# A row-sum kernel whose first load is split over even and odd partitions

## The chip, the core and the metric

The kernel runs on one core of a Trainium2 chip. The metric is device time in microseconds (us) of one execution; where several executions are given, their median counts. Lower is better. One further execution was recorded by the hardware profiler, and all views below come from that one.

## The reference

```python
def setup_inputs():
    batch, seq, dim = 32, 512, 1024
    return {"x": np.random.randn(batch, seq, dim).astype(np.float32)}

def reference(x):
    return np.sum(x, axis=-1).astype(np.float32)
```

The input is 32 x 512 = 16,384 rows of 1,024 float32 numbers, 67.1 MB. The output has one sum for each row, 64 KB. There is one addition for each number read, so the input has to pass from device memory (HBM) into the on-chip memory once, and little else has to be done.

## The kernel before

The on-chip memory has 128 partitions. Each partition gets 128 rows: `J = 128` columns in the tile `sums`, one for each row. The rows are in two blocks. `x_a`, the first 128 x 16 rows, gives partition p its rows 16p to 16p+15; `x_b`, the remaining 128 x 112, gives it 112 rows in one piece. `rows_from(j, n)` picks n neighbouring rows of every partition out of one of the two, so that a load reads, for each partition, one piece of n x 4 KB that lies in one place in HBM.

All loads are issued by SyncE (SP), in this order:

- seven rows per partition (`FIRST = 7`, columns 112 to 118 of `sums`), 28 KB for each partition, from `x_a`. This is the load that the change touches. `issue_first_load_at_entry` takes the first SP load of the program, if it waits for nothing, and moves it ahead of SP's first drain in the entry block, so ahead of the barrier in which all engines meet;
- seven loads of 16 rows per partition (`BIG = 16`), 64 KB for each partition, into three buffers in turn (`inpool`, `bufs=3`);
- six rows, two rows and one row, the last row in two pieces of 560 and 464 numbers.

VectorE (DVE) sums a whole load in one `tensor_reduce` (`vec`, L152); the 16-row one takes 17.2 us while the next 16 rows take 19.4 us to arrive. Near the end ScalarE (ACT) takes some rows (`act`, L179), and DVE takes others with a form that folds a row in half (`halves`, L166).

Two things hold back the loads that follow the first one. The tile of the second load, `second`, gets a `memset` on DVE first (L213), and because the load writes the same bytes it waits for that. The third load waits, by `hold`, for the sum over the first one:

```python
hold(load, first, "no descriptors of later loads while the first ones start")
```

`hold(inst, until, reason)` adds nothing but a wait for a semaphore. `ready` (L206) is an ACT instruction on one column of a small tile; it makes ACT fetch its table early, and nothing in the kernel before waits for it.

The schedule is the order of the program text (`manual_schedule`). Every buffer is written again when the sum over it has been done, which the framework turns into waits of the SP queue.

Of the kernel before, what the change touches and what calls it, by code (L numbers as in the profile page):

```python
# [100 lines left out]
@with_exitstack  # L101
def kernel(
    ctx: ExitStack,
    tc: tile.TileContext,
    x: bass.AP,
    out: bass.AP,
):
    nc = tc.nc
    nc.at_finalize(issue_first_load_at_entry)
    nc.at_finalize(order_waits)  # L110
    nc.at_finalize(wait_for_the_store_at_the_clear)
    fp32 = mybir.dt.float32
    P = 128
    batch, seq, dim = x.shape
    rows = batch * seq
    J = rows // P
    BIG = 16

    LONG = J - BIG
    rows_in = x.flatten_outer_dims()
    rows_out = out.rearrange("b s -> (b s)")
    x_a = rows_in[: P * BIG].rearrange("(p j) d -> p j d", p=P)
    x_b = rows_in[P * BIG :].rearrange("(p j) d -> p j d", p=P)
    out_a = rows_out[: P * BIG].rearrange("(p j) -> p j", p=P)
    out_b = rows_out[P * BIG :].rearrange("(p j) -> p j", p=P)


    def rows_from(j, n):
        return x_b[:, j : j + n, :] if j < LONG else x_a[:, j - LONG : j - LONG + n, :]

    last = 0
    FIRST = 7
    pieces = (560, 464)
    LINE = 64

    with (
        tc.tile_pool(name="small", bufs=1) as smallpool,  # L140
        tc.tile_pool(name="in", bufs=3) as inpool,
        tc.tile_pool(name="unread", bufs=4, space=bass.MemoryType.PSUM) as upool,
        tc.tile_pool(name="stage", bufs=1) as stpool,
        tc.manual_schedule(),
    ):


        seed = smallpool.tile([P, LINE // 2], fp32)
        sums = stpool.tile([P, J], fp32)

        def vec(dst, src):
            return nc.vector.tensor_reduce(  # L152
                out=dst, in_=src, axis=mybir.AxisListType.X, op=mybir.AluOpType.add
            )

        def hold(inst, until, reason):
            tc.add_manual_dep(
                inst.ins,
                until.ins.name,
                mybir.DependencyInfo(mybir.DependencyClass.Sync, mybir.DependencyReason.DATA),  # L160
                reason=reason,
            )

        def halves(dst, src):
            n = src.shape[-1] // 2
            return nc.vector.tensor_tensor_reduce(  # L166
                out=src[:, :n],
                in0=src[:, :n],
                in1=src[:, n:],
                scale=1.0,  # L170
                scalar=0.0,
                op0=mybir.AluOpType.add,
                op1=mybir.AluOpType.add,
                accum_out=dst,
            )

        def act(dst, src, n):
            unread = upool.tile([P, dim], fp32)
            nc.scalar.activation(  # L179
                out=unread[:, :n],  # L180
                in_=src,
                func=mybir.ActivationFunctionType.Copy,
                accum_out=dst,
            )

        sums_of = []

        def rows(t, a, n, j, n_act, pairs=False):
            nv = n - n_act
            block = t[:, a * dim : (a + n) * dim].rearrange("p (n d) -> p n d", d=dim)  # L190
            load = nc.sync.dma_start(out=block, in_=rows_from(j, n))  # L191
            if pairs:
                for q in range(nv):
                    sums_of.append(halves(sums[:, j + q : j + q + 1], block[:, q, :]))
            else:
                sums_of.append(vec(sums[:, j : j + nv], block[:, :nv, :]))
            for q in range(nv, n):
                act(sums[:, j + q : j + q + 1], block[:, q, :], dim)
            return load

        def store(eng, dst, j0, j1):
            return eng.dma_start(out=dst, in_=sums[:, j0:j1])

        nc.vector.memset(seed[:, :1], 0.0)  # L204
        unread = upool.tile([P, dim], fp32)
        ready = nc.scalar.activation(  # L206
            out=unread[:, :1], in_=seed[:, :1], func=mybir.ActivationFunctionType.Copy
        )

        j = last  # L210
        t = inpool.tile([P, BIG * dim + LINE], fp32)
        second = inpool.tile([P, BIG * dim + LINE], fp32, name="t")
        nc.vector.memset(second[:, : 4 * dim], 0.0)  # L213
        rows(t, 0, FIRST, j, 0)
        first = sums_of[-1]
        wholes = [LONG, *range(BIG, LONG, BIG)]
        for k, at in enumerate(wholes):
            t = second if k == 0 else inpool.tile([P, BIG * dim + LINE], fp32)
            if k < len(wholes) - 1:
                load = rows(t, 0, BIG, at, 0)  # L220
            else:
                rows(t, 0, BIG, at, 7, pairs=True)
            if k == 1:
                hold(load, first, "no descriptors of later loads while the first ones start")

        t = inpool.tile([P, BIG * dim + LINE], fp32)
        rows(t, FIRST, 6, j + FIRST, 2, pairs=True)
        two = rows(t, FIRST + 6, 2, j + FIRST + 6, 1, pairs=True)
        a = BIG - 1

        j += a
        c, width = pieces
        whole = t[:, a * dim + c : BIG * dim + 2]
        nc.vector.memset(whole[:, width + 1 :], 0.0)  # L234
        part = t[:, a * dim : a * dim + c]
        nc.sync.dma_start(out=part, in_=rows_from(j, 1)[:, 0, :c])  # L236
        nc.sync.dma_start(out=whole[:, :width], in_=rows_from(j, 1)[:, 0, c:])
        late = "its packets come behind those of the loads"
        hold(store(nc.scalar, out_b[:, BIG:], BIG, LONG), two, late)
        hold(store(nc.scalar, out_a, LONG, J), two, late)  # L240
        halves(whole[:, width : width + 1], part)
        halves(sums[:, j : j + 1], whole)
        store(nc.sync, out_b[:, :BIG], 0, BIG)
# [30 lines left out]
```

## Time and profile before

| What | Value |
|---|---|
| Time, median of 3 runs | 161.35 us (161.17 to 161.35) |
| Time of the profiled execution | 161.16 us |
| Its span in the profile | 159.4 us |
| DVE busy | 124.1 us (78%) |
| ACT busy | 12.1 us (8%) |
| HBM read | 67.11 MB, mean 421 GB/s over the span |
| First load (seven rows, 3,584 KB) | lands 10.7 us after its issue |

The profiled execution took 161.16 us, of which its span of 159.4 us begins with SP's issue of the first load; 1.8 us lie outside the span. A name such as `t<-in_x_dram` says what is written and what is read. An entry with a q behind the engine (SPq) belongs to that engine's sequencer, which issues DMAs and waits, and not to its arithmetic.

### The profile page before, as it was taken

The numbers are of one execution on the slowest core, as the hardware profiler recorded it, in microseconds if no ns is written. First come the engines' busy times: TensorE is split into PE (matmuls) and PEld (weight loads), VectorE is DVE, ScalarE is ACT, GpSimd is POOL, SyncE is SP. The second block draws the span as 40 slices with busy tenths as digits, with TensorE's granted clock in tenths as the row PEclk, the third lists the DMA queues.
The fourth block names the chain that finished last, engine by engine and source line by source line (L and its number), as shares of the span: only waits on it lengthen the run. The fifth ranks groups of instructions, "written<-read, shape, count | busy, mean of one in ns | idle before, by whom it ended". The sixth has DMA issues, their size and how long they took to land.

```text
span 159.4 us, 137 instructions
## 1 busy us (share of the span) xinstructions
DVE 124.1 (78%) x42; ACT 12.1 (8%) x22; POOL 0.2 (0%) x4
## 2 busy tenths in 40 slices
DVE  5339600499985999779995899949999499994955
ACT  3000000000000000000000000000000000003993
POOL 0000000000000000000000000000000000000000
DMA  9899999699699699699699797996996996995984
GB/s 324 374 486 526 395 395 526 280 510 526 263 526 526 263 526 526 263 526 526 263 526 461 329 526 313 477 526 263 526 526 263 526 526 263 526 526 247 444 371 139
DMA packets 2160, 67.18 MB, mean 421 GB/s; under 512 B 624, under 2 KB 752, under 8 KB 880
## 3 DMA queue, kind: packets, MB, share of 16 engines
q1 hardware_dynamic: 1872, 67.12, 97.9%
q10 hardware_dynamic: 288, 0.06, 0.2%
HBM read 67.11 MB, written 0.07 MB: 421 GB/s over the span
## 4 chain that ended last, share of the span: by engine, by line
DMA 71%; DVE 27%; SPq 1%; issue 0%; DVEq 0%
DMA t<-in_x_dram 71%; DVE sums L152 26%; SPq L191 0%; SPq L236 0%; DVE t L166 0%; DVEq L269 0%
## 5 line engine op out<-in xcount | busy, mean ns | idle before, releaser
L152 DVE TENSOR_REDUCE sums<-t 128x16 f32<-128x16384 f32 (+1 forms) x7 | 110.9, 15849 | 27.9 <-DMA t<-in_x_dram 27.9
L179 ACT ACTIVATE unread<-t 128x1024 f32<-128x1024 f32 x10 | 10.1, 1010 | 144.1 <-DMA t<-in_x_dram 144.1
L166 DVE CUSTOM_DVE_ANT_0 t<-t 128x512 f32<-128x512 f32 (+2 forms) x16 | 9.6, 656 | 4.0 <-DMA t<-in_x_dram 4.0
L213 DVE MEMSET t<- 128x4096 f32 x1 | 3.5, 3472 | 0.8 <-issue 0.8
L179 ACT ACTIVATION_READ_ACCUMULATOR unread<-t 128x1 f32 x10 | 1.9, 186 | 0.0
L206 ACT ACT_TABLE_LOAD x1 | 1.3, 1283 | 0.8 <-PEq L258 0.8
L166 DVE DVE_READ_ACCUMULATOR2_ANT sums<- 128x1 f32 x15 | 1.2, 83 | 0.0
L204 DVE MEMSET seed<- 128x1 f32 x1 | 0.1, 59 | 0.9 <-PEq L258 0.9
L206 ACT ACTIVATE unread<-seed 128x1 f32<-128x1 f32 x1 | 0.2, 174 | 0.0
L258 POOL MEMSET const-bfloat16-1.0<- 128x1 bf16 x1 | 0.1, 102 | 0.0
L258 POOL MEMSET const-uint8-127<- 128x1 uint8 x1 | 0.1, 102 | 0.0
L258 POOL MEMSET const-float32-0.0<- 128x1 f32 x1 | 0.1, 99 | 0.2 <-issue 0.2
L258 POOL MEMSET const-float32-1.0<- 128x1 f32 x1 | 0.1, 99 | 0.0
L166 DVE DVE_READ_ACCUMULATOR2_ANT t<- 128x1 f32 x1 | 0.1, 82 | 0.0
L234 DVE MEMSET t<- 128x1 f32 x1 | 0.1, 59 | 0.0
## 6 DMA issues: line engine op xcount, KB each, us to landing
t<-in_x_dram SPq DMA_DIRECT2D x1, 3584.0 KB, 10.7
t<-in_x_dram SPq DMA_DIRECT2D x1, 3072.0 KB, 28.7
t<-in_x_dram SPq DMA_DIRECT2D x1, 1024.0 KB, 30.8
t<-in_x_dram SPq DMA_DIRECT2D x1, 280.0 KB, 31.0
t<-in_x_dram SPq DMA_DIRECT2D x1, 232.0 KB, 31.1
t<-in_x_dram SPq DMA_DIRECT2D x7, 40.7
out_dram<-sums ACTq DMA_DIRECT2D x1, 48.0 KB, 1.6
out_dram<-sums ACTq DMA_DIRECT2D x1, 8.0 KB, 1.5
```

What stands on the lines that cost most here:

```text
L152: return nc.vector.tensor_reduce(out=dst, in_=src, axis=mybir.AxisListType.X, op=mybir.AluOpType.add)
L166: return nc.vector.tensor_tensor_reduce(out=src[:, :n], in0=src[:, :n], in1=src[:, n:], scale=1.0, scalar=0.0, op0=mybir.AluOpType.add, op ...
L179: nc.scalar.activation(out=unread[:, :n], in_=src, func=mybir.ActivationFunctionType.Copy, accum_out=dst,)
L204: nc.vector.memset(seed[:, :1], 0.0)
L206: ready = nc.scalar.activation(out=unread[:, :1], in_=seed[:, :1], func=mybir.ActivationFunctionType.Copy)
L213: nc.vector.memset(second[:, : 4 * dim], 0.0)
L234: nc.vector.memset(whole[:, width + 1 :], 0.0)
L258: nc = _bacc.Bacc("TRN2", target_bir_lowering=False, num_devices=1)
```

## The change

The load of the first seven rows becomes two: one over partitions 0, 2, 4 and so on, one over partitions 1, 3, 5 and so on, each with 64 pieces of 28 KB. The even one is the first SP load of the program now and waits for nothing, so it is the one that goes ahead of the barrier. The odd one waits for `ready`. The sum over the seven rows stays one instruction over all 128 partitions and so waits for both loads. In SP's order the odd load stands between the even one and the first 16-row load; nothing else moves on any engine.

```diff
         j = last
         t = inpool.tile([P, BIG * dim + LINE], fp32)
+        block = t[:, : FIRST * dim].rearrange("p (n d) -> p n d", d=dim)
+        source = rows_from(j, FIRST)
+        nc.sync.dma_start(out=block[0::2], in_=source[0::2])
+        odd = nc.sync.dma_start(out=block[1::2], in_=source[1::2])
+        hold(odd, ready, "no second load while the first one's descriptors are made")
         second = inpool.tile([P, BIG * dim + LINE], fp32, name="t")
         nc.vector.memset(second[:, : 4 * dim], 0.0)
-        rows(t, 0, FIRST, j, 0)
-        first = sums_of[-1]
+        first = vec(sums[:, j : j + FIRST], block)
+        sums_of.append(first)
         wholes = [LONG, *range(BIG, LONG, BIG)]
```

## The prediction

> **What bounds the kernel now.** I read the page first, for who is busy and which chain ends last.
>
> ```profile
> span 159.4 us, 137 instructions
> DVE 124.1 (78%) x42; ACT 12.1 (8%) x22; POOL 0.2 (0%) x4
> ...
> DMA  9899999699699699699699797996996996995984
> ...
> DMA t<-in_x_dram 71%; DVE sums L152 26%; SPq L191 0%; SPq L236 0%; DVE t L166 0%; DVEq L269 0%
> ```
>
> The chain's 26% of DVE does not make DVE a limit. The sixes in the DMA row come of how packets of 2.4 us fall into slices of 4 us. Windows that are long against a packet show the true rate, and the chain in order of time shows where both ends lie:
>
> ```profile
> 0.00:1.00 1.00, 0.06 (x1) 0.22 (x1) 0.20 (x4) 1.00 0.00 0
> 1.00:2.00 1.00, 0.26 (x1) 1.00 (x1) 0.00 (x0) 1.00 1.67 459
> 30.00:150.00 120.00, 107.14 (x19) 3.82 (x7) 0.00 (x0) 1.00 0.99 427
> ```
>
> ```profile
> 0.00 10.73 DMA t<-in_x_dram
> 10.73 0.02 issue
> 10.75 7.63 DVE sums L152
> ...
> 126.08 31.10 DMA t<-in_x_dram
> 157.18 0.02 issue
> 157.21 0.40 DVE t L166
> ```
>
> The last two columns of the first view are the DMA engines' busy share and GB/s: nothing moves in the first microsecond, then the 16 engines are full (0.99, 427 GB/s). The packet records of the trace say the same more finely. Every packet of the first load but the 16 first ones took 1.062 us for 28,672 bytes, every 16-row packet 2.418 us for 65,536: 27 GB/s an engine, back to back. All load packets together, divided by 16, make 155.8 us, from the first packet at 1.01 us to the last end at 156.8 us. So the time is: start of the first packet, plus 155.8 us of full engines, plus a tail. Only the first term, or a hole in the second, can change. The change works on the first. Three more views give its rows: the tile's instructions in the first microsecond, the same over the whole span, and the timeline.
>
> ```profile
> L191 SPq DMA_DIRECT2D t<-in_x_dram x1: 381/381/381, 0.0 to 0.0; - x1
> ```
>
> ```profile
> L191 SPq DMA_DIRECT2D t<-in_x_dram x10: 327/328/436, 0.0 to 125.1; - x10
> ...
> L236 SPq DMA_DIRECT2D t<-in_x_dram x1: 477/477/477, 125.6 to 125.6; - x1
> ```
>
> ```profile
> 0.78 1.28 ACT L206 ACT_TABLE_LOAD   x1 [0.78 <-PEq L258]
> ...
> 1.74 3.47 DVE L213 MEMSET t<- 128x4096 f32 x1 [0.82 <-issue]
> 2.08 0.17 ACT L206 ACTIVATE unread<-seed 128x1 f32<-128x1 f32 x1
> 10.75 7.62 DVE L152 TENSOR_REDUCE sums<-t 128x7 f32<-128x7168 f32 x1 [5.54 <-DMA t<-in_x_dram]
> ```
>
> The first issue took SP 0.381 us. Of the 16 engines, 15 start their first packet between 1.01 and 1.26 us (one is recorded at 1.88), and all end it between 2.64 and 2.98, 1.46 to 1.93 us after those starts where 1.062 us would do. That is the whole opening: 0.38 us of issue, 0.63 us from its end to the first packet, 0.25 us of spread between engines, some 0.6 us until data flow.
>
> **The change part by part.**
>
> The even load's issue. Every DMA of the trace is over 128 partitions at a step of one, so no row shows an issue over 64 at a step of two. By its nearest row, the first load's own 0.381 us, it costs nothing more; the issue does not look at size (0.327 us for 64 KB a partition, 0.347 for the 64 B of the last store), so a gain from half the bytes has no support. There is a reason for a loss: in the built programs all 15 DMAs of before carry a flag for a ready-made issue (`ant_dge_precooked`), and the two half loads are the only ones of the changed program without it. What that is worth no row shows. I bound it by nothing and by one more issue of the same length, +0.38 us, and take the middle, +0.20 us, all of it on the path, as everything later queues behind the first packet.
>
> Half the descriptors ahead of the first packets. If descriptors are made engine after engine, the spread of 0.25 us is their making, and half of them halves it: the last engine gains 0.12 us, the mean one 0.06. If all must be made before any packet starts, half of the 0.63 us is the end of what could go, -0.32 us. If the delay is fixed, nothing. Against the large value speaks the data flow: the first packets do not end in the order in which they start (one runs from 1.02 to 2.89 us, the last starter from 1.26 to 2.82), so the flow waits for something else than the making. I take -0.06. [...]
>
> One more load. Each engine gets one more completion packet, 9 ns in the records and some 6 ns around it: +0.015 us. When the second load was issued at 5.2 us, the packets running then took up to 1.069 us in place of 1.062; the odd load's descriptors do that once more over two packets: +0.015 us.
>
> The odd load's wait. It is released by `ready` at 2.25 us (later by what the even issue is longer, as SP's drain in the barrier stands behind that issue). With an issue of 0.38 to 0.76 us and 0.63 us to the packet it is there by 3.3 to 3.8 us. The even load keeps the engines busy until 1.0 + 0.6 + 4 x 1.06 = 5.9 us. So the wait costs nothing under a cover of some 2 us; every microsecond beyond it would be a hole in all engines and go to the end in full. Queued behind the waiting instruction on SP is the second load. It waits for the memset that ends at 5.21 us, so it is not moved by an odd issue that is over by 3.2; if the barrier is 0.2 us later, so are the memset and it, and its packets are wanted at 10.05 us. DVE's sum needs both completions and begins where the second comes, near 10.75; it ends near 18.4, and the third load behind it is wanted at 29.4. Both hide under the second load's 19.4 us.
>
> Sum: 0.20 - 0.06 + 0.015 + 0.015 = +0.17 us, from 161.16 us of the profiled execution to 161.33. That execution lies 0.19 us under the median of the runs, 161.35, and a median is what is compared: 161.5. The bounds of the terms, -0.32 + 0.03 and 0.38 + 0.03, give 161.05 to 161.75. A measurement of this kernel can tell about 0.2%, 0.32 us, from no change, so this forecast is "no change that can be told", on its late side.
>
> **The rivals.**
>
> The issue becomes the price (slower). Place: SP's first instruction. If the even load's issue takes 0.75 us or more, the start moves by over 0.32 us even with the 0.06 taken off, and the end with it, as nothing behind the first packet has slack. With an issue of 0.8 to 1.0 us: +0.36 to +0.59 us with the other terms, 161.7 to 161.95. For it: the missing flag, and full engines that cannot catch up. Against: all 15 issues of the trace lie between 0.33 and 0.48 us.
>
> The descriptors were the price (faster). The even load's issue is no longer than 0.38 us, the making is half, and packets had waited for all of it: -0.32 - 0.12 + 0.03 = -0.41 us, 160.95. For it: the opening is the one place where the engines idle. Against: the mixed order of ends, and 0.85 us from issue to first packet even for the last store with its 64 B a partition.
>
> Engines share a way into the partitions (much slower). With steps of two, an engine's four pieces may lie where another engine writes too. Two on one way at 27 GB/s make each of the eight first packets cost 1.062 us more: +8.5 us, 169.85, or half of that, 165.6, if only one of the loads suffers. The trace shows each engine at one steady pace in every load, so the 128-partition layout has no such sharing, and nothing on a step of two. [...]
>
> That nothing happens, with a fixed delay and an equal issue, is +0.03 us and part of the forecast's case.
>
> **How the numbers follow.** Forecast's case, the start moved by less than 0.32 us either way: 0.48. Long issue: 0.34, as the missing flag is the one definite difference between the programs. Descriptors: 0.10. Shared ways: 0.08. So faster 0.10, same 0.48, slower 0.34 + 0.08 = 0.42. The range takes in the first three, 160.9 to 161.95, and leaves out the sharing and the far ends of a long issue. The likeliest case alone: 161.05 to 161.65.
>
> **What would show it.** In the changed kernel's trace: SP's first issue against 0.381 us (0.58 expected; 0.75 or more is the first rival); first packets at 1.1 to 1.3 us with half the spread between engines (the second rival: 0.6 to 0.7 us); eight packets an engine of 1.062 us without a hole at 5.9 us (the third: 2.1 us each); both halves landed near 10.9 us; the later chain the same, shifted as a whole. A hole between the even and the odd packets, or a tail of another length, would make the prediction wrong in a way that I give no chance of its own.

## The result, and the profile after

The changed kernel takes 162.09 us (median of 5 runs, 161.90 to 162.56) against 161.29 us: a ratio of 1.0051 with an interval of 1.0035 to 1.0067. It is slower by 0.8 us, where 0.17 us and "no change that can be told" were forecast, and it lies above the range. One line of the description of the kernel needs setting right first: the kernel has `last = 0`, so the seven rows of the first load are rows 0 to 6 of `x_b` and fill columns 0 to 6 of `sums`; the pieces of 28 KB are as described, and no figure depends on it. The profiled execution took 162.17 us; its page begins:

```profile
span 160.4 us, 140 instructions
DVE 124.2 (77%) x42; ACT 12.1 (8%) x22; POOL 0.2 (0%) x4
...
DMA  7999699699699699699799799798997996996993
...
DMA 70%; DVE 26%; ACT 1%; SPq 1%; issue 0%; DVEq 0%
```

The last line has the shares by engine of the chain that ended last. The busy times are those of before. One entry is new in the chain's shares, ACT with 1%. The chain in order of time, the tile's instructions in the first microsecond, and the timeline show the opening:

```profile
1.19 1.28 ACT L206
2.47 0.01 issue
2.48 0.18 ACT unread L206
2.67 0.01 issue
2.68 8.62 DMA t<-in_x_dram
...
126.86 31.30 DMA t<-in_x_dram
158.16 0.04 issue
158.21 0.40 DVE t L166
```

```profile
L214 SPq DMA_DIRECT2D t<-in_x_dram x1: 549/549/549, 0.0 to 0.0; - x1
```

```profile
2.68 0.48 SPq L215 DMA_DIRECT2D t<-in_x_dram  x1
5.65 0.34 SPq L191 DMA_DIRECT2D t<-in_x_dram  x1
11.40 7.62 DVE L152 TENSOR_REDUCE sums<-t 128x7 f32<-128x7168 f32 x1 [5.78 <-DMA t<-in_x_dram]
```

The even load's issue takes 0.549 us (0.381 before). SP's drain behind it takes 0.362 us (0.132), so the barrier opens 0.40 us later, and `ready` lets the odd load go at 2.68 us. The chain runs through ACT and the odd load now.

The last fold starts at 158.21 us against 157.21, 1.0 us later in this pair of executions. The packet records split that, by the packet that is last at each point:

- The first packet starts at 1.33 us, not 1.01: +0.31 us.
- The seven rows' last packet ends at 11.00 us, not 10.40. So another +0.29 us goes at the boundary: two engines take 1.54 and 1.48 us for their first odd packet in place of 1.06.
- The last 16-row packet ends at 146.72 us, not 145.80: +0.31 us more in the 16-row loads. There 78 of 896 packets take 20 ns or more over 2.418 us, up to 0.13 us more (before: 20, none over 0.03). I call the sum of what all 16-row packets take over 2.418 us, divided by 16 engines, the excess: 0.37 us, against 0.14 before. So the excess explains 0.22 of these 0.31 us; it is an average over the engines, and the last engine lost more.
- Some 0.1 us is left for the loads behind them.

Averaged over the engines instead, the boundary costs only some 0.06 us.

### The profile page after: what moved, and what is told of

It is laid out like the page before. It is cut to its first block, busy times and chain, and to the rows that moved or that the text cites. A ratio compares the mean times of both kernels' runs of the same rounds, so it can differ in the third digit from the quotient of the medians.

```text
span 160.4 us, 140 instructions
## 1 busy us (share of the span) xinstructions
DVE 124.2 (77%) x42; ACT 12.1 (8%) x22; POOL 0.2 (0%) x4
## 4 chain that ended last, share of the span: by engine, by line
DMA 70%; DVE 26%; ACT 1%; SPq 1%; issue 0%; DVEq 0%
DMA t<-in_x_dram 70%; DVE sums L152 26%; ACT L206 1%; SPq L191 0%; SPq L241 0%; DVE t L166 0%; ACT unread L206 0%; DVEq L152 0%; DVEq L274 0%
```

## The experiments

Each kernel was timed against the kernel before on the same chip; "over" is the difference of the medians. Theory A: the longer issue is the price. Its first rival: a second load or its boundary is.

**The issue by itself.** The kernel before, with the flag for the ready-made issue taken from its first load.

```diff
         assert not load.sync_info.on_wait
+        load = copy.replace(load, ant_dge_precooked=False)
```

> The kernel before, with its one first load over all 128 partitions, but without the flag for the ready-made issue on that load. Theory A (the issue is the price): SP's first issue takes about 0.55 us as in the changed kernel (0.381 before), the drain behind it 0.36, the first packet starts near 1.33 us, and the time is 0.3 us over before; what else the changed kernel lost (0.8 us in all) stays away. Theory B (the half partitions and the second load are the price, the flag is worth nothing): 0.381 us, first packet near 1.01, time of before within 0.1 us.

Measured: 161.55 us, 0.31 over (ratio 1.0017, 1.0008 to 1.0026), excess 0.15 us.

```profile
L192 SPq DMA_DIRECT2D t<-in_x_dram x1: 550/550/550, 0.0 to 0.0; - x1
```

The flag is worth 0.17 us of issue, 0.23 us of the drain behind it (0.367 us) and 0.31 us of first packet: 1.33 us here as in the changed kernel. That is theory A, for 0.3 of the 0.8 us. The number of pieces is worth nothing, as 128 pieces without the flag start when 64 do.

**Two loads without partition steps.** Four and three rows over all partitions.

```diff
-        nc.sync.dma_start(out=block[0::2], in_=source[0::2])
-        odd = nc.sync.dma_start(out=block[1::2], in_=source[1::2])
+        nc.sync.dma_start(out=block[:, :4], in_=source[:, :4])
+        odd = nc.sync.dma_start(out=block[:, 4:], in_=source[:, 4:])
```

> Two first loads over all 128 partitions, of four rows and of three, both flagged, the second one waiting for the same ACT instruction as the odd load. Theory A: first issue 0.38 us, first packet near 1.01 us, time within 0.1 us of before. Theory B (a second load at this place costs by itself, at the boundary between the two, where two engines of the changed kernel took 1.5 us in place of 1.06 for their first odd packet): some engines stall by 0.4 us at the boundary, time 0.3 to 0.5 us over before.

Measured: 161.39 us, 0.15 over (0.9998 to 1.0016), first packet at 0.99 us. So a second load with a wait on `ready` is not dear by itself, as theory A had it.

**The changed kernel again, and before again.**

> The changed kernel once more. In its first profile single 16-row packets all over the run took 0.02 to 0.13 us too long, which before did not show, and the last load landed 0.4 us later than the first loads' delay explains. Theory A (these are an accident of that execution): they are not there again, the profile lies nearer to 0.6 us over before, and the median 0.5 to 0.8 over. Theory C (they come from the change, for instance from engines that are out of step): they are there again, at about the same size.

> The kernel before once more, for a second profile of it on the chip of these runs. Theory A: if this chip or hour makes long packets, they are here too, and then belong to no kernel. Theory C: none are here, as in the first profile of before (first packet near 1.01 us, last load landed near 157.2 us).

Measured: 162.10 us, 0.86 over, and 161.20 for before. The excess is 0.68 us in the changed kernel and 0.13 in before, so theory A's "accident" falls: the long packets belong to the change. The timeline of the changed kernel, again, shows them adding up; in brackets is DVE's idle time. Then the same of before:

```profile
30.75 17.22 DVE L152 TENSOR_REDUCE sums<-t 128x16 f32<-128x16384 f32 x1 [11.72 <-DMA t<-in_x_dram]
50.37 17.22 DVE L152 TENSOR_REDUCE sums<-t 128x16 f32<-128x16384 f32 x1 [2.40 <-DMA t<-in_x_dram]
69.92 17.22 DVE L152 TENSOR_REDUCE sums<-t 128x16 f32<-128x16384 f32 x1 [2.33 <-DMA t<-in_x_dram]
89.32 17.22 DVE L152 TENSOR_REDUCE sums<-t 128x16 f32<-128x16384 f32 x1 [2.18 <-DMA t<-in_x_dram]
```

```profile
30.17 17.22 DVE L152 TENSOR_REDUCE sums<-t 128x16 f32<-128x16384 f32 x1 [11.80 <-DMA t<-in_x_dram]
49.42 17.22 DVE L152 TENSOR_REDUCE sums<-t 128x16 f32<-128x16384 f32 x1 [2.03 <-DMA t<-in_x_dram]
68.81 17.22 DVE L152 TENSOR_REDUCE sums<-t 128x16 f32<-128x16384 f32 x1 [2.17 <-DMA t<-in_x_dram]
88.15 17.22 DVE L152 TENSOR_REDUCE sums<-t 128x16 f32<-128x16384 f32 x1 [2.12 <-DMA t<-in_x_dram]
```

From one of these sums to the next, a load takes 19.4 to 19.6 us in place of 19.3 to 19.4.

**Both row-wise loads without the flag.** The two loads of the second experiment; a function run on the built program takes the flag from both (the other loads have other lengths).

```diff
+            if isinstance(i, mybir.InstDMACopy) and i.engine == mybir.EngineType.SP and i.outs[0].ap[1][1] in (4096, 3072):
+                insts[k] = copy.replace(i, ant_dge_precooked=False)
```

> The two first loads of four and of three rows over all 128 partitions, now both without the flag, as the two half loads are. The changed kernel loses 0.3 us by its longer issue and some 0.5 us more, for which its two profiles show 16-row packets that take up to 0.3 us too long. Theory D (the 0.5 us come from the loads over 64 partitions at a step of two): time 0.3 us over the flagged two loads, near 161.7, the 16-row packets at 2.418 us throughout (excess over that, summed over all and divided by 16 engines, about 0.13 us as in before). Theory E (they come from a second load without the flag, issued while the first one runs): near 162.1, excess 0.4 to 0.7 us as in the changed kernel.

Measured: 161.66 us, 0.42 over, excess 0.08 us. The 0.3 us of the issue are there, the long packets are not; theory E falls.

**The wait taken away.**

```diff
         odd = nc.sync.dma_start(out=block[1::2], in_=source[1::2])
-        hold(odd, ready, "no second load while the first one's descriptors are made")
```

> The changed kernel without the odd load's wait, so that it is issued right behind the barrier. Theory D: the wait is not the price, time as the changed kernel, near 162.1, long packets as there. Theory F (the odd load's descriptors come at a bad moment, while the second packets run, and throw the engines out of step): another moment, another loss; time moves by 0.2 us or more either way and the spread between engines at the end of the seven rows changes with it (0.42 to 0.73 us in the two profiles of the changed kernel, 0.35 to 0.38 in before).

Measured: 161.57 us, 0.33 over (1.0013 to 1.0030), excess 0.12 us. Its timeline:

```profile
1.19 0.48 SPq L215 DMA_DIRECT2D t<-in_x_dram  x1
...
30.62 17.22 DVE L152 TENSOR_REDUCE sums<-t 128x16 f32<-128x16384 f32 x1 [11.70 <-DMA t<-in_x_dram]
49.89 17.22 DVE L152 TENSOR_REDUCE sums<-t 128x16 f32<-128x16384 f32 x1 [2.05 <-DMA t<-in_x_dram]
69.22 17.22 DVE L152 TENSOR_REDUCE sums<-t 128x16 f32<-128x16384 f32 x1 [2.10 <-DMA t<-in_x_dram]
```

Issued 1.5 us earlier, the odd load costs nothing beyond the issue: the other 0.5 us are the wait's, which moves the load, as theory F had it in the main. Theory D falls, as the loads over every other partition are all here.

**Halves in place of even and odd.**

```diff
-        nc.sync.dma_start(out=block[0::2], in_=source[0::2])
-        odd = nc.sync.dma_start(out=block[1::2], in_=source[1::2])
+        nc.sync.dma_start(out=block[:64], in_=source[:64])
+        odd = nc.sync.dma_start(out=block[64:], in_=source[64:])
```

> The first load split into partitions 0 to 63 and 64 to 127 in place of even and odd. Theory of shared ways (engines that write to the same eighth of the partitions share one way at 27 GB/s): packets of the first loads take about 2.1 us in place of 1.06, and the time is up to 8.5 us over before; the even and odd split, whose packets kept 1.06 us, is then a layout that avoids it. If no ways are shared: time as the changed kernel, near 162.1.

Measured: 170.33 us (170.22 to 170.34 in three executions, 192.61 in a fourth), 9.1 over. The packets of both loads take 2.24 us at the median. The windows, first of halves and then of the changed kernel, with GB/s last:

```profile
2.00:18.00 16.00, 3.47 (x1) 0.65 (x2) 0.00 (x0) 1.00 0.99 204
```

```profile
2.00:10.00 8.00, 3.47 (x1) 0.64 (x2) 0.00 (x0) 1.00 0.95 405
```

The halves move at half the rate of the even and odd loads, which keep 1.06 us a packet at the median, as the single load of before does. The theory of shared ways forecast about 2.1 us a packet for the halves. That engines share a way was not shown by itself; no other reason for the rate was tried.

**Quarters.** Four loads over every fourth partition, the second with the wait.

```diff
+        nc.sync.dma_start(out=block[0::4], in_=source[0::4])
+        for q in range(1, 4):
+            odd = nc.sync.dma_start(out=block[q::4], in_=source[q::4])
+            if q == 1:
+                hold(odd, ready, "...")
```

> The first load in four over every fourth partition, 32 pieces each, the second one waiting for the ACT instruction, the others behind it. Theory D (a partition step above one sets off the long packets): they are there, time 162.1 or later. Descriptor theory: the first packets start earlier than the 1.33 us of the 64-piece load by up to 0.1 us if the number of pieces is made before they start; if the issue is all, again 1.33 us and 0.55 us of issue.

Measured: 162.30 us, 1.06 over, excess 0.27 us, an issue of 0.54 us and the first packet at 1.33 us. Theory D forecast that time too, but it fell with the run without the wait. Without the flag, 32, 64 and 128 pieces alike have their first packet at 1.33 us.

**The odd load's moment.** A part of the memset (64 or 1,500 columns) releases it. The lead is the time from the issue of a load until the packets of the load before it end.

```diff
+        second = inpool.tile([P, BIG * dim + LINE], fp32, name="t")
+        gate = nc.vector.memset(second[:, :64], 0.0)
         odd = nc.sync.dma_start(out=block[1::2], in_=source[1::2])
-        hold(odd, ready, "no second load while the first one's descriptors are made")
-        second = inpool.tile([P, BIG * dim + LINE], fp32, name="t")
-        nc.vector.memset(second[:, : 4 * dim], 0.0)
+        hold(odd, gate, "no second load while the first one's descriptors are made")
+        nc.vector.memset(second[:, 64 : 4 * dim], 0.0)
```

> The changed kernel with the odd load released by the first 64 columns of the memset on DVE, near 2.2 us, in place of the ACT instruction (issued at 2.7 us in the changed kernel, at 1.2 us without the wait). Without the wait the time was 161.57 us and the long 16-row packets were gone; with it 162.1. Theory J (the odd load must be there some 3.5 us before the even one's packets end near 6.0 us, because the engines read ahead of what they write): a lead of 3.8 us in place of 3.3, so a time between the two, 161.6 to 161.9. Theory K (the wait itself is the price, or any issue while data flow): as the changed kernel, 162.1.

> The same with 1,500 columns of the memset, so that the odd load is issued near 3.5 us. Theory J: a lead of 2.5 us; every engine stalls at the boundary, by 0.3 to 0.8 us, and the time is 162.4 to 162.9. Theory K: 162.1 as the changed kernel, since its packets are wanted only near 6.0 us and 1.9 us pass from issue to flow.

Measured: 161.84 us (0.57 over, excess 0.12, issued at 1.45 us, earlier than I had reckoned) and 162.43 us (1.16 over, excess 0.37, issued at 2.95 us). In both, 0.27 us more than usual lie outside the span (2.06 us against 1.79), which the last section takes up; without them they stand 0.30 and 0.89 over. The issues of the two:

```profile
1.45 0.48 SPq L217 DMA_DIRECT2D t<-in_x_dram  x1
```

```profile
2.95 0.48 SPq L217 DMA_DIRECT2D t<-in_x_dram  x1
```

Theory K falls by the first: the wait has no price of its own, its moment has. The second decides nothing. Only the 0.27 us outside the span put it into theory J's range; its span is that of the changed kernel, 160.4 us, and its lead is nearly the same. Nor did every engine stall: four took 0.19 to 0.33 us too long for their first odd packet, and one stood still for 0.25 us.

**The second row-wise load late.** Four rows, then three, the second load released by the whole memset.

```diff
+        nc.sync.dma_start(out=block[:, :4], in_=source[:, :4])
+        gate = nc.vector.memset(second[:, : 4 * dim], 0.0)
         odd = nc.sync.dma_start(out=block[:, 4:], in_=source[:, 4:])
-        hold(odd, ready, "...")
+        hold(odd, gate, "...")
```

> The two first loads of four and three rows over all 128 partitions with the flag, the second one released by the whole memset, near 5.25 us in place of 2.26. The first one's packets end at 6.3 to 7.1 us in its earlier profile, so the lead is 1.1 to 1.8 us. Theory J: a hole between the two loads of 0.5 to 1 us in all engines and long 16-row packets after it, time 161.9 to 162.5: lateness alone does it, at any partition step. Theory L (only loads at a step of two set off long packets): a hole, but 16-row packets at 2.418 us (excess under 0.15 us) and the time over the 161.39 us of the early release by the hole alone.

Measured: 161.73 us, 0.46 over, excess 0.09 us. In its profiled execution (162.12 us) the loss is at the boundary: packets of the second load take up to 0.62 us too long, 0.37 us an engine on average, and the engines stand still by 0.11 us at most. So there is no hole, which both theories expected. The 16-row packets are clean, which theory J did not expect and theory L did.

**Three tries at the long packets.** A tiny extra load over the even partitions of a spare tile; an extra load into partitions 0 to 7; and four rows over all partitions, followed by three rows over the even and the odd ones.

```diff
+        spare = smallpool.tile([P, 16], fp32)
+        extra = nc.sync.dma_start(out=spare[0::2], in_=rows_from(j, 1)[0::2, 0, :16])
+        hold(extra, ready, "while the first load's packets run")
```

```diff
+        nc.sync.dma_start(out=t[:8, 8 * dim : 9 * dim], in_=rows_from(j, 1)[:8, 0, :])
```

```diff
+        nc.sync.dma_start(out=block[:, :4], in_=source[:, :4])
+        even = nc.sync.dma_start(out=block[0::2, 4:], in_=source[0::2, 4:])
+        hold(even, ready, "while the first load's packets run")
+        nc.sync.dma_start(out=block[1::2, 4:], in_=source[1::2, 4:])
```

> The kernel before with its one first load, and one tiny extra load of 64 B into each even partition of a spare tile (64 pieces, not needed for the result), issued when the ACT instruction is done, while the first load's packets run, as the odd load is in the changed kernel. Theory M (descriptors of a load over every other partition, written while data flow, set off the long packets): excess of the 16-row packets 0.3 us or more, time 161.6 to 161.9. Theory P (they come of how the engines stand to each other after the boundary between even and odd): no boundary with a stall here, excess under 0.15 us, time within 0.1 us of before.

> The kernel before with an extra load of 4 KB into each of partitions 0 to 7, behind the first load and not needed for the result, which puts some of the engines behind the others by 0.15 to 0.6 us. Theory P: the engines stand otherwise to each other than in before, long packets follow, excess 0.3 us or more and the time over before by 0.3 us more than the delay that the end of the first two loads shows. Theory M: no step of two, excess under 0.15 us, the time over before by that delay alone.

> Four rows over all 128 partitions with the flag, then three rows over the even and three over the odd partitions, both issued from 2.3 us on, while the first four rows' packets run until 6.3 us or later. Leads of 3 to 4 us, more than the odd load has in the changed kernel. Theory M: long packets, excess 0.3 us or more, time 161.7 to 162.0. Theory J (lead alone decides): excess under 0.15 us, time near the 161.39 us of the two row-wise loads.

Measured: 161.55 us (0.30 over, excess 0.11), 161.37 us (0.12 over, excess 0.14) and 161.32 us (0.07 over, 0.9997 to 1.0014, excess 0.07). Theory M falls twice: loads over every other partition, issued at 2.26 and 2.84 us while data flow, cost nothing when what runs lasts until 6.5 us. Theory P has no support. The tiny load's 0.30 us was foreseen by neither and stays unexplained. In its profile the engines end the first load's packets 0.66 us apart, against 0.35 in before; they are that far apart from the end of their first packets on, at 2.66 to 3.32 us, and the tiny packets themselves take 0.04 us.

**The lead by itself.** Eleven first rows in place of seven, in the changed kernel and in before (the tail's load of six rows becomes one of two).

```diff
-    FIRST = 7
+    FIRST = 11
```

> The changed kernel with eleven first rows in place of seven (the tail has two rows in place of six to match), so that the even load's packets last until about 8.6 us while the odd load is issued at 2.7 us as before: a lead of 5.9 us in place of 3.3. Theory J (the lead decides): no long packets, excess of the 16-row packets under 0.15 us, time 0.3 us over the single load of eleven rows. Theory Q (issuing the odd load while the even one runs is the price, whatever the lead): long packets, time 0.6 to 0.9 us over the single load of eleven rows.

> The single first load with eleven rows, the measure for the run above. Both theories: near the time of before, 161.2 to 161.5 us, as the tail is short of work on all engines but DMA; excess under 0.15 us.

Measured: 164.56 and 164.19 us, excess 0.09 and 0.12 us. With eleven rows the kernel is slower in itself, against what I expected: in the second run the last data arrive at 156.97 us (156.82 in before), but ACT is busy with its rows until 160.6. What is lost ahead of the last 16-row load still reaches the end, as DVE and ACT wait for it. The pair's difference is 0.37 us. The odd load is issued as in the changed kernel and costs nothing but the issue:

```profile
2.69 0.48 SPq L215 DMA_DIRECT2D t<-in_x_dram  x1
```

At the front nothing else differs from the changed kernel but the length of the pieces, 44 KB in place of 28, and with it how long the even load lasts (until 8.68 us in place of 6.03). Theory Q falls, theory J stands.

**Short leads elsewhere.** The row-wise load and the pair behind four rows, released by a part of the memset (3,200 and 2,600 columns).

```diff
+        gate = nc.vector.memset(second[:, :3200], 0.0)
+        odd = nc.sync.dma_start(out=block[:, 4:], in_=source[:, 4:])
+        hold(odd, gate, "no second load while the first one's descriptors are made")
```

> Four and three rows over all 128 partitions with the flag, the second one issued near 3.9 us, with a lead of some 2.4 us in place of 4.1 (early) or 1.1 (late). Theory J with partial stalls: some engines run dry at the boundary and others not, long packets follow as in the changed kernel, excess 0.25 us or more, time 161.7 to 162.2. Theory R (only loads over half the partitions can do it): excess under 0.15 us, time between the 161.39 of the early and the 161.73 of the late release.

> Four rows over all partitions, then three rows over the even and over the odd ones, issued near 3.4 us in place of 2.3: a lead of some 3.0 us, as short as in the changed kernel. Theory J and theory R: the long packets are there, excess 0.25 us or more, time 161.7 to 162.2 against 161.32 with the early release. Theory Q: as with the early release, 161.3, since both are issued while the first load runs.

Measured: 162.86 us (1.56 over, excess 0.02) and 162.65 us (1.35 over, excess 0.03); 1.29 and 1.08 over without the 0.27 us outside the span. The loads went out at 4.29 and 3.67 us, some 0.3 us later than I had reckoned. The windows of the first of them, then of the same loads released early:

```profile
4.00:10.00 6.00, 1.06 (x2) 0.00 (x0) 0.00 (x0) 1.00 0.98 360
```

```profile
4.00:10.00 6.00, 1.20 (x1) 0.00 (x0) 0.00 (x0) 1.00 1.01 433
```

A short lead is dear with all partitions and the flag, too: single packets of the second load take up to 1.23 us too long, and one engine stands still for 0.63 us. But the loss lies at the boundary, and the 16-row packets are clean. In the second kernel both theories J and R expected long packets, and they are not there either. So a short lead costs time in all the layouts here, as theory J has it in the main, and the form that the cost takes follows neither theory.

The kernels with a second early load, by lead, taken here until the first engine has done with the load before it ("net": without the 0.27 us outside the span). The halves, with another packet rate, and the two extra loads, which carry nothing that is needed, are left out. Issue, lead and excess are of the one profiled execution:

| Kernel | Issued | Lead | Excess | Over before, net |
|---|---|---|---|---|
| even/odd of eleven rows | 2.69 | 6.0 | 0.09 | 0.37 over its single load |
| even/odd, no wait | 1.19 | 5.0 | 0.12 | 0.33 |
| even/odd, 64 columns | 1.45 | 4.7 | 0.12 | 0.30 |
| rows, then even/odd | 2.26 | 4.2 | 0.07 | 0.07 |
| rows, no flag | 2.68 | 4.1 | 0.08 | 0.42 |
| rows | 2.26 | 4.1 | 0.10 | 0.15 |
| **changed kernel** (and again) | 2.68 | 3.3 (3.6) | 0.37 (0.68) | 0.80 (0.86) |
| even/odd, 1,500 columns | 2.95 | 3.2 | 0.37 | 0.89 |
| rows, then even/odd, mid | 3.67 | 2.8 | 0.03 | 1.08 |
| rows, mid | 4.29 | 2.1 | 0.02 | 1.29 |
| quarters | 2.67 | 1.5 | 0.27 | 0.79 |
| rows, late | 5.24 | 1.2 | 0.09 | 0.46 |

With 4.1 us of lead or more, nothing is lost but the 0.3 us of a missing flag on the first load, within 0.15 us. With 3.6 us or less something always is. The layouts on the two sides of that line differ; in one layout alone, even/odd of seven rows, the step lies between 3.6 and 4.7 us.

## Why the prediction was wrong, point by point

**What bounds the kernel** held: full engines from the first packet to the last (a DMA share of 0.99 from 30 to 150 us, before and after), and the losses at the front and in packets reached the end. "Every 16-row packet 2.418 us" is the most frequent value; they take up to 2.446 us in before, which makes its excess of 0.14 us.

**The even load's issue** was the right mechanism and somewhat undersized: +0.20 us was put, with bounds from 0 to 0.38; it is 0.31, shown by the flag alone. The issue itself grew by 0.17; the first packet came another 0.15 us later, from a cause that the records do not show. SP's drain behind the issue grew too, by 0.23 us, and delayed the barrier and with it the odd load.

**Half the descriptors** (-0.06) is nothing. The spread of the first packets, which half the descriptors should have halved, is 0.32 us against 0.25 (one engine left out in each). The faster rival, which needed them to be the price, is out.

**One more load** (two times 0.015 us) was not resolved; the rows-then-even/odd run, with two more loads, is 0.07 us over before and not told from it.

**The odd load's wait** is the step that failed: "the wait costs nothing under a cover of some 2 us". I had put the issue of the odd load at 2.25 us and a bit, its packets "there by 3.3 to 3.8 us" and wanted at 5.9, as if an engine wanted its next packet only when the last one ends. Issued at 2.68 us, the odd load ought by that to have had 1.9 us to spare (2.68 + 1.33 = 4.0 us). The runs show that it has to be issued earlier: leads of 3.3 to 3.6 us lose 0.5 us, leads of 4.7 us nothing. Without the wait the kernel took 161.57 us, inside the range; the wait is what took it out. What I had called a hole "in all engines" was 0.42 and 0.48 us in two engines' packets, and a scatter of long 16-row packets until 144 us. A hole between the even and the odd packets was named as a sign of being wrong, with no chance of its own; for the long packets the prediction had no case.

**The long-issue rival** was not what happened: its point of decision, an issue of 0.75 us, was not reached (0.55), though the start moved by 0.31 us, just under the 0.32 that it names. That the time came out near this rival's (161.7 to 161.95 us) is chance, as 0.5 of the 0.8 us are the wait's. Its +0.36 us, by the other terms, should read +0.39; nothing hangs on that. The sharing rival (+8.5 us) comes near what the halves lose, 9.1 us, and is wrong for this change, whose 28 KB packets keep 1.06 us at the median. Its chance of 0.08 was my estimate; the profile of before has no load at a step of two.

**Left open.** That the odd load's moment decides, and not its wait or its form, is shown by the run without the wait, the eleven-row pair and the load released by 64 columns. How is not. That engines read ahead of what they write, the reason that theory J gives, was my guess; no run showed it. Long 16-row packets (excess 0.27 to 0.68 us) follow a short lead where the first load of all is over half or a quarter of the partitions; where it is over all of them, a short lead costs only at the boundary, even if half loads come next. Why is not explained. Engines out of step are not the reason by themselves: the row-wise load in the middle has a spread of 0.98 us between engines all through its 16-row loads, and no long packets. Nor is it explained why a wholly late load (lead 1.2 us, 0.46 over) costs less than one half late (2.1 us, 1.29 over), nor why an extra load of 64 B a partition costs 0.30 us.

## What to carry to other kernels

Where the DMA engines never rest (a share of 0.99 here), a load that is held back must be issued well before the queue ahead of it runs out: here 4.1 us were enough and 3.6 us were not, in different layouts, though issue and first packet account for only 1.3 us. So judge such a wait by runs at several moments and not by the arithmetic of latencies. A split that changes a load's shape can change the cost of issuing it: for the first load here the issue took 0.55 us in place of 0.38, and the first packet came 0.31 us later; the missing flag alone cost 0.31 us of the time. If a load has to be split by partitions, use every other partition and not the halves (162.09 against 170.33 us here).

## What the runs showed of the hardware

- Without the flag the first load's issue took 0.55 us in place of 0.38, the drain behind it 0.36 in place of 0.13, and the first packet came at 1.33 us in place of 1.01. It came then with 32, 64 and 128 pieces alike.
- The changed kernel's long packets, up to 0.13 us too long in one profile and 0.32 us in the other, are scattered over the 16-row loads, the last at 144 us. These loads are the same in every kernel, and the only change is some 140 us before, at the front.
- Five kernels (quarters, and the four with the memset in two) show 2.06 us outside the span, all others 1.78 to 1.80. In the records these five alone have 54 entries on DVE, and the others 53 or fewer. That is an observation; the cause was not tried.
